# Token sums of a hybrid decoder layer taken from whole copies, two more pairs as block steps, weight sums and banks in another order

## The chip, the core and the metric

One Trainium2 chip, one core. The kernel is a whole decoder layer for 512 tokens, in float32. The time is that of the device for one execution, in microseconds (us); a median of three runs is given, and one further execution was profiled. TensorE (PE) multiplies, VectorE (DVE) and ScalarE (ACT) work on rows of up to 1024 elements in 128 partitions, GpSimd (POOL) does small things, SyncE (SP) issues most of the transfers. SBUF is the memory on the chip from which the engines read, PSUM the eight banks of 128x512 floats in which TensorE accumulates.

## What is computed

The reference, cut to what matters here:

```python
def rms_norm(x, g):
    y = x * lax.rsqrt(jnp.mean(x * x, axis=-1, keepdims=True) + RMS_EPS)
    return y * g

def swiglu(x, w_gate, w_up, w_down):
    return (jax.nn.silu(x @ w_gate) * (x @ w_up)) @ w_down

# the layer: x is 512 tokens x 1024, w_gate and w_up 1024 x 2816, w_down 2816 x 1024
x = x + 0.5 * rms_norm(swiglu(rms_norm(x, ffn1_pre), ...), ffn1_post)
x = x + rms_norm(mixer(rms_norm(x, mix_pre), ...), mix_post)
x = x + 0.5 * rms_norm(swiglu(rms_norm(x, ffn2_pre), ...), ffn2_post)
```

The mixer (two kinds of attention and gates) is not touched but for its last step, where its result is normed for the second FFN.

## The kernel before

**Products.** A float32 operand is split into a high part of TensorE's reduced float32 format and the rest: `whi`, `wlo` for weights, `xh`, `xl` for tokens. ScalarE casts the high part, VectorE subtracts it for the rest (`split`, L104 to L107). One product is three matmuls (`mm3`, L127 to L131): high by high, high by rest, rest by high.

**An FFN's up part.** The 2816 columns of w_gate and w_up are 22 blocks of 128, taken as 11 pairs p. A classical pair (`classical`, L390) is four units (gate and up of two blocks) of 8 slices of 128 of the inner dimension, three matmuls of 512 tokens each: 96 matmuls of 512 columns. A block pair (`strassen`, L325) takes gate and up together by seven products of half size after Strassen and Winograd: 7 x 2 x 4 x 3 = 168 matmuls of 256 columns. It needs sums of the weights (S1 to S4, 128x1024 on VectorE, from the tiles `raw`, into tiles `tmp`) and, once for each FFN, four sums of the tokens T1 to T4 (`token_sums`, L471). `STRASSEN` says which pairs are block pairs: before, 3 to 10 in the first FFN and 2 to 10 in the second.

**Token sums before.** T1 to T4 are sums and differences of four quarters of the normed tokens. Each quarter is first put together again from its parts, xh + xl, on VectorE (`join`, L491, eight times 128x512 for an FFN), then summed and split. `STEPS` deals the steps out over the classical blocks, from block 1 on.

**The start of an FFN.** The tokens are normed in four tiles t of 128 (`norm_steps`, L187): a scale on VectorE into `tmp`, eight 128x128 transposes on TensorE into two PSUM banks, a cast of each bank on ScalarE (xh) and a rest on VectorE (xl). The first four units, called g0, u0, g1, u1 here, are done in halves: first the tokens of tiles 0 and 1 (256 columns), later those of tiles 2 and 3, so that they can start early.

**What sets the order.** In the opening (L1426 to L1481) the order on ScalarE, VectorE and TensorE is that in which the code is written, with a few transposes of the identity (`keep_busy`) between. Elsewhere a scheduler orders the instructions within each engine. Each engine then runs its queue in order. PSUM banks are named by tags S (three buffers), T (two), V (one) and F (two); a bank that is given out anew can be written when all that read it have run. The tiles `raw`, into which weights are loaded, have three buffers, and a load starts when its buffer's last readers are done.

## Time and profile before

| what | before |
|---|---|
| median of 3 runs | 1138.97 us (1138.95 to 1139.98) |
| the profiled execution, its time | 1138.51 us |
| its span (first to last instruction) | 1136.4 us |
| TensorE busy | 1119.9 us, 6921 instructions |
| VectorE busy | 908.0 us, 1563 instructions |
| ScalarE busy | 638.0 us, 1145 instructions |
| pairs 0 to 10 of the first FFN, second halves on | from 26.69 us |
| second FFN, first matmul with its tokens | at 795.40 us |
| its pair 1 and pair 2, first matmul to first matmul | 820.46 to 842.24 and 842.24 to 862.40 us |

The times in a profile are counted from the start of the span. An entry of a timeline shows the start, the duration, the engine, the line of the kernel, the operation with output and input, and in brackets how long the engine stood idle before it and what ended that. Durations overlap a little, because an engine starts the next instruction before the last one has quite ended; so the distance from start to start is what one instruction costs in a row.

### The profile page before, as it was taken

How to read it: one execution, taken by the hardware profiler on the slowest of the kernel's cores; microseconds unless marked ns; L12 is line 12 of the kernel's file. 1: busy time of each engine (PE TensorE's matmuls, PEld its weight loads, DVE VectorE, ACT ScalarE, POOL GpSimd, SP SyncE). 2: the span in 40 equal slices, each digit the busy share in tenths (PEclk: the TensorE clock that was granted, in tenths of full speed). 3: DMA queues.
4: the chain of work that ended last, by engine and by line, in shares of the span. 5: the costliest groups of instructions: out<-in, count | busy, mean ns of one | idle time of the engine just before them, and what ended most of it. 6: DMA issues, size and time to landing. Idle time of an engine off the chain costs nothing.

```text
span 1136.4 us, 18463 instructions
## 1 busy us (share of the span) xinstructions
PE 1119.9 (99%) x6921; PEld 999.5 (88%) x6921; DVE 908.0 (80%) x1563; ACT 638.0 (56%) x1145; POOL 78.3 (7%) x112
## 2 busy tenths in 40 slices
PE   8999999999999999999999999999999999999997
PEld 7889999998878987778888998788989999998885
DVE  6989999878667889687665687976878888979665
ACT  5435555566464688687565635644445555558552
POOL 1000000000022032343000000001000000000001
PEclk9999999999999999999999999999999999999999
DMA  9995665578655552111476758683133433357753
GB/s 321 331 307 187 190 199 186 154 265 295 220 184 148 172 134 85 53 41 56 142 248 224 251 176 293 207 301 107 66 121 121 130 98 129 109 181 236 280 189 115
DMA packets 152908, 206.01 MB, mean 181 GB/s; under 512 B 19794, under 2 KB 97906, under 8 KB 152564
## 3 DMA queue, kind: packets, MB, share of 16 engines
q1 hardware_dynamic: 152816, 204.85, 55.1%
q8 instruction: 54, 0.88, 0.3%
q14 instruction: 34, 0.28, 0.1%
q10 hardware_dynamic: 4, 0.00, 0.0%
HBM read 165.45 MB, written 39.37 MB: 180 GB/s over the span
## 4 chain that ended last, share of the span: by engine, by line
PE 88%; DVE 6%; ACT 2%; DMA 1%; issue 1%; POOL 1%; SPq 0%; POOLq 0%; DVEq 0%; ACTq 0%
PE pb_F L131 11%; PE pb_F L129 11%; PE pb_F L130 11%; PE pb_S L131 8%; PE pb_S L130 8%; PE pb_S L129 8%; PE pb_T L130 6%; PE pb_T L131 6%; PE pb_T L129 6%; PE pb_V L130 3%; PE pb_V L129 3%; PE pb_V L131 3%; PE pb_V L986 2%; PE pb_T L971 1%; DVE SP_s L721 1%
## 5 line engine op out<-in xcount | busy, mean ns | idle before, releaser
L106 ACT CAST whi<-raw 128x1024 fp32r<-128x1024 f32 (+2 forms) x221 | 225.4, 1020 | 260.3 <-issue 68.2
L107 DVE TENSOR_TENSOR wlo<-raw,whi 128x1024 fp32r<-128x1024 f32 (+2 forms) x221 | 261.3, 1185 | 103.6 <-ACT whi L106 99.7
L129 PE MATMUL pb_F<-xh_t,whi 128*128 128x512 f32 (+1 forms) x392 | 142.6, 364 | 0.6 <-ACT whi L106 0.4
L131 PE MATMUL pb_F<-xh_t,wlo 128*128 128x512 f32 (+1 forms) x392 | 141.6, 361 | 0.5 <-DVE wlo L107 0.5
L130 PE MATMUL pb_F<-xl_t,whi 128*128 128x512 f32 (+1 forms) x392 | 141.9, 362 | 0.0
L106 ACT CAST whi<-tmp_t 128x1024 fp32r<-128x1024 f32 x51 | 53.5, 1048 | 61.0 <-PE pb_S L130 22.0
L131 PEld LDWEIGHTS pb_F<-xh_t,wlo 128*128 128x128 f32 x392 | 74.1, 189 | 10.8 <-DVE wlo L107 1.0
L129 PEld LDWEIGHTS pb_F<-xh_t,whi 128*128 128x128 f32 x392 | 74.1, 189 | 10.6 <-ACT whi L106 0.6
L130 PEld LDWEIGHTS pb_F<-xl_t,whi 128*128 128x128 f32 x392 | 74.2, 189 | 9.7
L107 DVE TENSOR_TENSOR wlo<-tmp_t,whi 128x1024 fp32r<-128x1024 f32 x51 | 62.4, 1223 | 25.2 <-ACT whi L106 23.9
L129 PE MATMUL pb_S<-xh_t,whi 128*128 128x256 f32 (+1 forms) x240 | 73.2, 305 | 0.0
L131 PE MATMUL pb_S<-xh_t,wlo 128*128 128x256 f32 (+1 forms) x240 | 73.0, 304 | 0.0
L130 PE MATMUL pb_S<-xl_t,whi 128*128 128x256 f32 (+1 forms) x240 | 73.0, 304 | 0.0
L151 POOL TENSOR_TENSOR rs_t<-rs_t,mhalf_t 128x1 f32<-128x1 f32 x24 | 19.2, 798 | 546.4 <-DVE rs_t L147 546.4
L130 PE MATMUL pb_T<-xl_t,whi 128*128 128x256 f32 (+1 forms) x184 | 53.9, 293 | 0.0
L129 PE MATMUL pb_T<-xh_t,whi 128*128 128x256 f32 (+1 forms) x184 | 53.9, 293 | 0.0
L131 PE MATMUL pb_T<-xh_t,wlo 128*128 128x256 f32 (+1 forms) x184 | 53.8, 292 | 0.0
L962 POOL TENSOR_SCALAR SP_s<-SP_s,st_t 128x384 f32<-128x384 f32 (+2 forms) x48 | 45.7, 968 | 106.5 <-DVE st_t L898 80.5
L130 PEld LDWEIGHTS pb_S<-xl_t,whi 128*128 128x128 f32 x240 | 45.9, 191 | 1.9
L129 PEld LDWEIGHTS pb_S<-xh_t,whi 128*128 128x128 f32 x240 | 45.9, 191 | 1.9
L131 PEld LDWEIGHTS pb_S<-xh_t,wlo 128*128 128x128 f32 x240 | 45.9, 191 | 1.9
L107 DVE TENSOR_TENSOR PT_s<-pb_T,PT_s 128x512 fp32r<-128x512 f32 (+1 forms) x72 | 39.2, 559 | 6.1 <-ACT PT_s L106 5.5
(808 smaller groups left out, 3350.6 us busy)
## 6 DMA issues: line engine op xcount, KB each, us to landing
raw<-in_ffn_w_up_dram SPq DMA_DIRECT2D x36, 512.0 KB, 5.2
raw<-in_w_in_dram SPq DMA_DIRECT2D x18, 1024.0 KB, 5.4
raw<-in_ffn_w_gate_dram SPq DMA_DIRECT2D x35, 512.0 KB, 4.7
raw<-tdram SPq DMA_DIRECT2D x16, 1024.0 KB, 5.2
raw<-in_ffn_w_down_dram SPq DMA_DIRECT2D x14, 1024.0 KB, 5.7
NN_s<-in_ffn_w_down_dram SPq DMA_DIRECT2D x22, 512.0 KB, 5.1
tdram<-NN_s SPq DMA_DIRECT2D x22, 512.0 KB, 3.9
raw<-tdram SPq DMA_DIRECT2D x8, 768.0 KB, 5.9
```

Source lines behind the costliest of these rows:

```text
L106: self.last_cast = self.nc.scalar.copy(dsthi, src).ins
L107: self.last_rest = self.nc.vector.tensor_sub(dstlo, src, dsthi.bitcast(F32)).ins
L129: mm(out, lhi, rhi, start=start, stop=False, skip_group_check=skip)
L130: mm(out, lhi, rlo, start=False, stop=False, skip_group_check=skip)
L131: mm(out, llo, rhi, start=False, stop=stop, skip_group_check=skip)
L151: nc.gpsimd.tensor_tensor(out=r, in0=v, in1=self.mhalf, op=OP.pow)
L721: nc.vector.tensor_tensor_reduce(p, s, w, -1.0, FLOOR, OP.add, OP.min, st_m)
L962: nc.gpsimd.tensor_scalar(pp, pp, st[:, 1, t:t + 1], None, op0=OP.mult)
L971: nc.tensor.transpose(b[:, o + (t - kk) * P:o + (t - kk + 1) * P], pt[pn][:, po + kk * P:po + (kk + 1) * P], self.ident)
L986: self.nc.tensor.matmul(out[:, kk * P:S], v, pp, start=first and kk == 0 and pi == 0, stop=False, skip_group_check=True)
```

## The change

Five things are changed.

1. **Whole copies.** In the opening and at the end of the mixer ScalarE copies each transposed bank into a slot as it stands (`full`, 128x256 twice for each bank, 16 copies for an FFN), tiles 0 and 1 into slots V and tiles 2 and 3 into slots x. The token sums are made from these copies, and the eight joins of each FFN go.
2. **Two more block pairs**: pair 2 in the first FFN, pair 1 in the second. The token sums are begun at block 0 instead of block 1, and `STEPS` deals them out faster.
3. **Weight sums in another order**: S3 = A11 - A21 first, S2 = A22 - S3, S1 = S2 + A11, then S4. Before, S1 = A21 + A22 came first, S2 = S1 - A11.
4. **Banks of pair 2 of the second FFN** are given out in another order.
5. The second FFN's count of banks starts at 3 instead of 7.

```diff
--- before.py
+++ after.py
@@ -44,14 +44,16 @@
 SPLIT_TAGS = dict(X=["Q"] * 4 + ["KA"] * 2, O=["V"] * 2 + ["KA"] * 2 + ["KB"] * 4 + ["SP"] * 11 + ["PT"] * 3,
                   Y=["PT"] * 5 + ["W"] * 2 + ["CB"] + ["Q"] * 4)
 T_TAGS = ["NN"] * 3 + ["N"] + ["PT"] * 8 + ["CB"]
-STRASSEN = range(3, NF // 2), range(2, NF // 2)
+STRASSEN = range(2, NF // 2), range(1, NF // 2)
 AHEAD = {0: 10, 1: 9}
 SUM_TAGS = {2: ["KB"] * 4, 3: ["x"] * 4, 4: ["x"] * 4, 5: ["V"] * 4, 6: ["x"] * 4, 7: ["V"] * 4,
             8: ["of"] * 2 + ["V"] * 2}
-STEPS = (0, 3, 3, 3, 3), (4, 4, 4)
+STEPS = (0, 4, 4, 4), (6, 6)
 HOLD_TAGS = ["W"] * 2 + ["Q"] * 4 + ["KA"] * 2 + ["V"] * 2 + ["CB", "ring"]
 PS_BUFS = dict(S=3, T=2, V=1, F=2)
 PS_TAGS = [t for t in PS_BUFS for _ in range(PS_BUFS[t])]
+
+WHOLE = "VV", "xx"
 
 OPEN = ("SS", "TT", "SS", "FF")
 AFTER_FFN, AFTER_MIX = ("SS", "FF", "SS", "TT"), ("SS", "TT", "FF", "SV")
@@ -63,6 +65,7 @@
         self.pool = ctx.enter_context(tc.tile_pool(name="sb", bufs=1))
         self.psum = ctx.enter_context(tc.tile_pool(name="ps", bufs=1, space=PSUM))
         self.nps = 0
+        self.whole = {}
         self.consts()
 
     def slot(self, tag, dt=F32, shape=(P, S)):
@@ -184,7 +187,10 @@
     def squares(self, t):
         return [self.meansq(x, S) for x in self.x[2 * t:2 * t + 2]]
 
-    def norm_steps(self, t, pre, tags):
+    def new_whole(self, half):
+        self.whole[half] = [[self.slot(tag).rearrange("p (k c) -> p k c", k=2) for _ in range(2)] for tag in WHOLE[half]]
+
+    def norm_steps(self, t, pre, tags, whole=False):
 
         nc = self.nc
         xn = self.sbt("tmp", [P, D], bufs=2)
@@ -207,12 +213,21 @@
         def rest(h):
             ks = slice(4 * h, 4 * h + 4)
             self.last_rest = nc.vector.tensor_sub(xl[:, ks, c], pt[h].rearrange("p (j c) -> p j c", j=4), xh[:, ks, c].bitcast(F32)).ins
-        return scale, transpose, cast, rest
-
-    def norm_T(self, t, pre, tags, sq=None):
+
+        def full(h):
+            if not whole:
+                return
+            if t % 2 == 0 and h == 0:
+                self.new_whole(t // 2)
+            for j in range(2):
+                o = self.whole[t // 2][h][j][:, :, (t % 2) * P:(t % 2 + 1) * P]
+                self.last_cast = nc.scalar.copy(o, pt[h][:, 2 * j * P:2 * (j + 1) * P].rearrange("p (j c) -> p j c", j=2)).ins
+        return scale, transpose, cast, rest, full
+
+    def norm_T(self, t, pre, tags, sq=None, whole=False):
 
         r = self.rstd(sq or self.squares(t))
-        scale, transpose, cast, rest = self.norm_steps(t, pre, tags)
+        scale, transpose, cast, rest, full = self.norm_steps(t, pre, tags, whole)
         for h in range(2):
             scale(h, r)
 
@@ -221,6 +236,8 @@
                 transpose(h)
                 cast(h)
                 rest(h)
+            for h in range(2):
+                full(h)
         return transposes
 
 
@@ -340,15 +357,16 @@
                  for i in (0, 4) for h in range(2)]
             b11, b21, b22 = x[0], x[2], x[3]
             t1, t2, t3, t4 = self.tsum
-            r12, r21, r11, r7 = [self.bank() for _ in range(4)]
-            nc.vector.tensor_add(s1, a21, a22)
+            banks = [self.bank() for _ in range(4)]
+            r12, r21, r11, r7 = [banks[i] for i in ((0, 3, 1, 2) if (n, p) == (1, 2) else range(4))]
             w = block(a11)
             nc.vector.tensor_sub(a21, a11, a21)
             product(r11, w, b11, True, False)
             w = block(a21)
             product(r7, w, t3, True, True)
-            nc.vector.tensor_sub(s2, s1, a11)
+            nc.vector.tensor_sub(s2, a22, a21)
             w = block(s2)
+            nc.vector.tensor_add(s1, s2, a11)
             nc.scalar.copy(r12, r11)
             product(r12, w, t2, False, False)
             w = block(a12)
@@ -400,11 +418,11 @@
                 bs.append(b)
             nc.scalar.activation(act, bs[0], AF.Silu)
             nc.vector.tensor_mul(act, act, bs[1])
-            if f == 1:
+            if f == 0:
                 sums.extend(self.token_sums())
-            if 1 <= f <= len(STEPS[n]):
+            if f < len(STEPS[n]):
                 with self.tc.issue_after(self.last_rest):
-                    for _ in range(STEPS[n][f - 1]):
+                    for _ in range(STEPS[n][f]):
                         sums.pop(0)()
 
         c = slice(0, H), slice(H, S)
@@ -472,7 +490,6 @@
 
 
         nc = self.nc
-        H = S // 2
         places = []
         for tag in T_TAGS:
             v = self.slot(tag, F32R, (P, D if tag == "NN" else S))
@@ -480,36 +497,27 @@
         self.tsum = [([], []) for _ in range(4)]
         steps = []
         for c in range(2):
-            hi, lo, whole = [[v.rearrange("p (k c) -> p k c", k=2) for v in g]
-                             for g in (places[8 * c:8 * c + 4], places[8 * c + 4:8 * c + 8],
-                                       [self.slot("x") for _ in range(4)])]
-            f1, f2, f3, f4 = whole
+            hi, lo = [[v.rearrange("p (k c) -> p k c", k=2) for v in g]
+                      for g in (places[8 * c:8 * c + 4], places[8 * c + 4:8 * c + 8])]
+            whole = f1, f2, f3, f4 = [self.whole[h][i][c] for i, h in ((0, 0), (1, 1), (0, 1), (1, 0))]
             for i in range(4):
                 for o, v in zip(self.tsum[i], (hi[i], lo[i])):
                     o.extend(v[:, k] for k in range(2))
 
-            def join(dst, i, h, c=c):
-                ks, cs = slice(4 * i + 2 * c, 4 * i + 2 * c + 2), slice(h * H, (h + 1) * H)
-                nc.vector.tensor_add(dst, self.xht[:, ks, cs].bitcast(F32), self.xlt[:, ks, cs].bitcast(F32))
-
             def sub(dst, x, y):
                 nc.vector.tensor_sub(dst, x, y)
 
             def parts(i, hi=hi, lo=lo, whole=whole):
                 self.split(hi[i], lo[i], whole[i])
 
-            def s1(f1=f1, f3=f3, join=join):
-                join(f3, 0, 1)
-                join(f1, 0, 0)
+            def s1(f1=f1, f3=f3):
                 sub(f1, f3, f1)
 
-            def s2(f1=f1, f2=f2, f3=f3, join=join):
-                join(f2, 1, 1)
+            def s2(f1=f1, f2=f2, f3=f3):
                 sub(f3, f2, f3)
                 sub(f2, f2, f1)
 
-            def s3(f2=f2, f4=f4, join=join):
-                join(f4, 1, 0)
+            def s3(f2=f2, f4=f4):
                 sub(f4, f4, f2)
 
             steps += [s1, s2, lambda p=parts: p(0), s3, lambda p=parts: (p(1), p(2)), lambda p=parts: p(3)]
@@ -1438,8 +1446,8 @@
             sq0 = [sq, self.meansq(self.x[1], S)]
             sq1 = self.squares(1)
             r0 = self.rstd(sq0)
-            scale0, transpose0, cast0, rest0 = self.norm_steps(0, g, OPEN[0])
-            scale1, transpose1, cast1, rest1 = self.norm_steps(1, g, OPEN[1])
+            scale0, transpose0, cast0, rest0, full0 = self.norm_steps(0, g, OPEN[0], True)
+            scale1, transpose1, cast1, rest1, full1 = self.norm_steps(1, g, OPEN[1], True)
             hi, lo = self.wpair([KT, P])
             src = self.pre_raw["g"][:, :, 0:P]
 
@@ -1473,15 +1481,19 @@
             cast1(1)
             rest1(1)
             self.pre_split = [self.ktiles(w) for w in ((hi, lo), self.wsplit(self.pre_raw["u"][:, :, 0:P], [KT, P]))]
+            full0(0)
             sq2 = self.squares(2)
+            full0(1)
             self.pre_split.append(self.ktiles(self.wsplit(self.pre_raw["g"][:, :, P:2 * P], [KT, P])))
-            t2 = self.norm_T(2, g, OPEN[2], sq2)
+            t2 = self.norm_T(2, g, OPEN[2], sq2, True)
+            full1(0)
             sq3 = self.squares(3)
+            full1(1)
             self.pre_split.append(self.wslots(self.pre_raw["u"][:, :, P:2 * P], "SP"))
-            t3 = self.norm_T(3, g, OPEN[3], sq3)
+            t3 = self.norm_T(3, g, OPEN[3], sq3, True)
         self.pending = [t2, t3]
 
-        def boundary(post, pre, store, tags=None):
+        def boundary(post, pre, store, tags=None, whole=False):
             def load():
                 return self.gains((post, pre))
 
@@ -1492,14 +1504,14 @@
                 if pre is not None:
                     if t == 0:
                         self.new_xT()
-                    self.pending.append(self.norm_T(t, gain, tags[t]))
+                    self.pending.append(self.norm_T(t, gain, tags[t], None, whole))
             return load, finish
 
         self.ffn(0, a["ffn1_w_gate"][0], a["ffn1_w_up"][0], a["ffn1_w_down"][0],
                  *boundary(a["ffn1_post"][0], a["mix_pre"][0], self.xdram, AFTER_FFN), a["x"][0], "TTSV", 6, self.distances)
-        self.mixer(*boundary(a["mix_post"][0], a["ffn2_pre"][0], self.x2dram, AFTER_MIX))
+        self.mixer(*boundary(a["mix_post"][0], a["ffn2_pre"][0], self.x2dram, AFTER_MIX, True))
         self.ffn(1, a["ffn2_w_gate"][0], a["ffn2_w_up"][0], a["ffn2_w_down"][0],
-                 *boundary(a["ffn2_post"][0], None, out), self.x2dram, "TTFS", 7)
+                 *boundary(a["ffn2_post"][0], None, out), self.x2dram, "TTFS", 3)
 
 
 _INS = ['x', 'ffn1_pre', 'ffn1_post', 'ffn1_w_gate', 'ffn1_w_up', 'ffn1_w_down',
```

How this moves the instructions is seen in the order on the engines. ScalarE in the opening, **before**, from the last cast of the first two tiles on; `xh_t` is the cast of tokens, `whi` that of weights (u0, then g1), ACTIVATE the squares of tiles 2 and 3, `SP_s` the cast of u1:

```order
L205 CAST xh_t<-pb_T 128x4x128
L106 CAST whi<-raw 128x1024
L138 ACTIVATE junk_t,ss_t<-x_s 128x512 x2
L106 CAST whi<-raw 128x1024
L138 ACTIVATE junk_t,ss_t<-x_s 128x512 x2
L106 CAST SP_s<-raw 128x512 x2
```

The same place **after**, where the COPY rows at L224 are the whole copies of tile 0 (from the banks S) and tile 1 (from the banks T):

```order
L211 CAST xh_t<-pb_T 128x4x128
L109 CAST whi<-raw 128x1024
L224 COPY V_s<-pb_S 128x2x128 x2
L141 ACTIVATE junk_t,ss_t<-x_s 128x512 x2
L224 COPY V_s<-pb_S 128x2x128 x2
L109 CAST whi<-raw 128x1024
L224 COPY V_s<-pb_T 128x2x128 x2
L141 ACTIVATE junk_t,ss_t<-x_s 128x512 x2
L224 COPY V_s<-pb_T 128x2x128 x2
L109 CAST SP_s<-raw 128x512 x2
```

Eight copies have come between the casts and the squares; the first copy out of a bank T stands behind the cast of g1.

TensorE at the first matmul of unit g0, with what each row waits for in brackets, **before** (the transposes of the identity at L1424 are those of `keep_busy`; the numbers name the buffers):

```order
L1424 MATMUL pb_V_90<-ident_t_61 128x128 x4
L129 MATMUL pb_T_226<-xh_t_88,whi_133 128x256 [waits DVE_49]
L130 MATMUL pb_T_226<-xl_t_89,whi_133 128x256
L131 MATMUL pb_T_226<-xh_t_88,wlo_134 128x256
L129 MATMUL pb_T_226<-xh_t_88,whi_133 128x256
```

and **after**:

```order
L1432 MATMUL pb_V_90<-ident_t_61 128x128 x4
L132 MATMUL pb_T_238<-xh_t_88,whi_133 128x256 [waits DVE_49,Activation_49]
L133 MATMUL pb_T_238<-xl_t_89,whi_133 128x256
L134 MATMUL pb_T_238<-xh_t_88,wlo_134 128x256
L132 MATMUL pb_T_238<-xh_t_88,whi_133 128x256
```

The rows are the same; the first matmul now waits for ScalarE's counter (Activation) as well as for VectorE's. The count that it waits for is reached with the second copy out of the bank T that the unit is given.

VectorE at the start of the second FFN, **before**: `rs_t` is a step of tile 3's norm, `tmp_t<-x_s,rs_t,CP_s` its two scales, `xl_t` the rests of tiles 2 (F) and 3 (S, V), and L493 the first joins.

```order
L147 TENSOR_SCALAR rs_t<-ss_t 128x1
L197 SCALAR_TENSOR_TENSOR tmp_t<-x_s,rs_t,CP_s 128x512 x2
L209 TENSOR_TENSOR xl_t<-pb_F,xh_t 128x4x128 x2
L209 TENSOR_TENSOR xl_t<-pb_S,xh_t 128x4x128
L209 TENSOR_TENSOR xl_t<-pb_V,xh_t 128x4x128
L493 TENSOR_TENSOR x_s<-xh_t,xl_t 128x512 x3
```

The same place **after**:

```order
L150 TENSOR_SCALAR rs_t<-ss_t 128x1
L363 TENSOR_TENSOR raw<-raw 128x1024
L203 SCALAR_TENSOR_TENSOR tmp_t<-x_s,rs_t,CP_s 128x512 x2
L367 TENSOR_TENSOR tmp_t<-raw 128x1024
L215 TENSOR_TENSOR xl_t<-pb_F,xh_t 128x4x128 x2
L215 TENSOR_TENSOR xl_t<-pb_S,xh_t 128x4x128
L215 TENSOR_TENSOR xl_t<-pb_V,xh_t 128x4x128
```

Two sums of weights have come into the sequence: pair 2's S3 (L363) ahead of tile 3's scales, and pair 1's S2 (L367) ahead of the rests.

## The prediction

> **What bounds the kernel now.** I read the page's busy line first, then the windows view of TensorE for the two long stretches in which the FFNs' up products run.
>
> ```profile
> PE 1119.9 (99%) x6921; PEld 999.5 (88%) x6921; DVE 908.0 (80%) x1563; ACT 638.0 (56%) x1145; POOL 78.3 (7%) x112
> ...
> 20.00:337.00 317.00, 316.56 (x2101) 1.00 0.70 233
> 803.00:1117.00 314.00, 314.00 (x2165) 1.00 0.45 150
> ```
>
> The columns of the lower rows are the stretch, its length, TensorE's busy time with its instruction count, granted clock, DMA share, GB/s. TensorE is busy 316.56 of 317 us and 314.00 of 314. So it sets the end nearly everywhere, and two things follow. A matmul that is removed from these stretches shortens the run by its whole length. And a pause that is put in ahead of them lengthens it by its whole length, since nothing behind it has room to catch up. The few gaps at the start therefore matter as much as the matmuls, and I looked at the timeline there next.
>
> **The gain: two pairs as block steps.** The change takes pair 2 of the first FFN and pair 1 of the second from the classical form (96 matmuls of 512 columns) to the block form (168 of 256). The second FFN runs one of each kind back to back, cut exactly at their first matmuls:
>
> ```profile
> 820.46:842.24 21.78, 21.78 (x98) 18.03 (x97) 17.08 (x24) 7.04 (x10) 0.00 (x0) 1.00 0.42 136
> 842.24:862.40 20.16, 20.16 (x170) 20.15 (x169) 17.61 (x20) 10.74 (x14) 0.00 (x0) 1.00 0.28 95
> ```
>
> Behind the length stand TensorE, weight loads, VectorE, ScalarE, GpSimd, clock, DMA share and GB/s. The classical pair takes 21.78 us, the block pair 20.16, with TensorE busy throughout in both. One pair gained is 1.62 us, two are **−3.2 us**. VectorE has 17.61 us of work in a block pair of 20.16, ScalarE 10.74, so in the steady state both stay hidden. The eight removed joins and the added copies of the token sums lie on these two engines and cost or gain nothing by themselves where TensorE does not wait for them. The reordered weight sums (S2 and S1 swap, one input is awaited less) are the same number of VectorE instructions per pair, so I put them at nothing; 2.5 us of slack per pair covers them.
>
> **The opening: the first matmul gets a new thing to wait for.** This is the term I found only by following the banks. Here is the opening of before, ScalarE and then TensorE (start, duration, line, operation, and in brackets the idle time ahead):
>
> ```profile
> 12.14 1.06 ACT L106 CAST whi<-raw 128x1024 fp32r<-128x1024 f32 x1
> 13.10 0.64 ACT L138 ACTIVATE junk_t<-x_s 128x512 bf16<-128x512 f32 x1
> ...
> 14.39 0.18 ACT L138 ACTIVATION_READ_ACCUMULATOR junk_t<-x_s 128x1 f32 x1
> 15.04 1.05 ACT L106 CAST whi<-raw 128x1024 fp32r<-128x1024 f32 x1 [0.46 <-DMA raw<-in_ffn_w_gate_dram]
> 15.99 0.62 ACT L138 ACTIVATE junk_t<-x_s 128x512 bf16<-128x512 f32 x1
> ```
> ```profile
> 11.43 0.60 PE L1424 MATMUL pb_V<-ident_t 128*128 128x128 f32 x4
> 12.03 0.39 PE L129 MATMUL pb_T<-xh_t,whi 128*128 128x256 f32 x1
> ...
> 18.00 0.28 PE L131 MATMUL pb_T<-xh_t,wlo 128*128 128x256 f32 x1
> 18.93 1.31 PE L202 MATMUL pb_S<-ident_t,tmp_t 128*128 128x128 f32 x8 [0.65 <-DVE tmp_t L197]
> ```
>
> The first unit accumulates in a bank T that held half of the second tile's transposes. In before, that bank is free when VectorE has taken its rest, and the matmul starts at 12.03, right behind the keep-busy transposes. After the change the copies of the whole sums read the same bank, and TensorE's first matmul waits on ScalarE too, for the second copy out of that bank. ScalarE works in order, and ahead of this copy now stand: the cast of u0 (ends so that the next starts at 13.10), two copies out of S, two squares, two more copies out of S, the cast of g1, then the two copies out of T.
>
> A copy of 128x256 out of PSUM by ScalarE has near relatives in before:
>
> ```profile
> L106 ACT CAST PT_s<-pb_T 128x256 fp32r<-128x256 f32 x32 | 11.5, 370 | 7.3 <-DVE PT_s L107 3.8 <-PE pb_T L1237 2.3 <-PE pb_T L971 1.0
> 382.08 0.70 ACT L106 CAST PT_s<-tmp_t 128x248 fp32r<-128x248 f32 x2
> ```
>
> One takes 0.37 us from PSUM; two of about this size, from SBUF, take 0.70 back to back (so they overlap by some 0.1). I take 0.65 for two, with 0.50 and 0.74 as ends. The walk along ScalarE: 13.10 + 0.65 = 13.75; the two squares last from 13.10 to 14.57 in before, 1.47, which gives 15.22; + 0.65 = 15.87 (the load of g1, which came at about 15.04, is there by now); the cast 15.04 to 15.99 is 0.95, so 16.82; + 0.65 = **17.5**. TensorE's first matmul starts 5.5 us later than 12.03.
>
> What of this comes back: the 48 matmuls in the two T banks ran from 12.03 to 18.12 and then waited 0.65 for the scaled tile 2. They would now take 5.8 to 6.1 us from 17.5, to 23.3 or 23.6. The second T bank's copies stand behind two more squares, at about 17.5 + 1.4 + 0.65 = 19.6, and are needed at 17.5 + 2.9 = 20.4, so they hold nothing. Tile 2's scale moves to about 20, earlier than needed. The transposes that started at 18.93 start at about 23.4: **+4.5 us** (4.0 with the low copy price, 4.8 with the high). From there TensorE has the same work as before, and no gap into which the delay could vanish.
>
> **The clock during that pause.** TensorE would sit idle for 5.5 us, from 12.03 on. The trace shows one such pause, behind the last matmul of the run, and the slow start of the run:
>
> ```profile
> 1129.56 0.39 PE L131 MATMUL pb_T<-whi,PT_s 128*128 128x512 f32 x1
> 1130.00:1134.00 4.00, 0.00 (x0) 0.00 (x0) 2.23 (x4) 0.69 (x2) 0.55 (x1) 1.00 0.31 115
> 1134.00:1136.40 2.40, 0.00 (x0) 0.00 (x0) 0.00 (x0) 0.00 (x0) 0.00 (x0) 0.52 0.30 114
> 6.69 1.97 PE L202 MATMUL pb_S<-ident_t,tmp_t 128*128 128x128 f32 x8 [0.41 <-DVE tmp_t L197]
> 10.85 0.75 PE L202 MATMUL pb_T<-ident_t,tmp_t 128*128 128x128 f32 x4
> ```
>
> The last matmul ends at 1129.95; the granted clock is 1.00 up to 1134 and 0.52 after it, which is half rate from about 1134.1, so 4.15 us after the last matmul. A pause of 5.5 us is longer than that, and the rate would fall at about 16.2. At the start, four transposes took about 1 us at 6.69 (eight in 1.97) and 0.75 at 10.85: some 4 us of nearly steady work until the full rate came. I take 3.9 us at half rate from 17.5, of which half is lost: **+1.9 us**. The ends are nothing (the rate stays) and 3.9 (two such stretches). This does not hang on the sum above.
>
> [...]
>
> **The start of the second FFN.** The copies of tiles 0 and 1 fall into idle time of ScalarE. But pair 2's block subtraction of the raw weights (which in before is pair 2's first sum too, and much later in VectorE's order since pair 1 was classical) now stands ahead of tile 3's scale.
>
> ```profile
> 794.72 0.38 SPq L335 DMA_DIRECT2D raw<-in_ffn_w_gate_dram  x1
> 795.17 0.49 SPq L335 DMA_DIRECT2D raw<-in_ffn_w_up_dram  x1
> raw<-in_ffn_w_gate_dram SPq DMA_DIRECT2D x1, 512.0 KB, 3.8
> raw<-in_ffn_w_up_dram SPq DMA_DIRECT2D x1, 512.0 KB, 5.8
> 800.19 0.21 DVE L147 TENSOR_SCALAR rs_t<-ss_t 128x1 f32<-128x1 f32 x1 [0.95 <-ACT junk_t L138]
> 801.13 1.41 DVE L197 SCALAR_TENSOR_TENSOR tmp_t<-x_s,rs_t,CP_s 128x512 f32<-128x512 f32 x2 [0.73 <-POOL rs_t L151]
> 802.03 0.60 PE L202 MATMUL pb_S<-ident_t,tmp_t 128*128 128x128 f32 x4
> 802.60 0.66 PE L202 MATMUL pb_V<-ident_t,tmp_t 128*128 128x128 f32 x4
> ```
>
> The load of that raw tile hangs on the same event as in before (the last rest of unit u1), is issued at 795.17 and lands 5.8 us later, at 801.0. The subtraction of 128x1024 takes about 1.15 us until the next instruction, so the scale starts at 802.15 instead of 801.13. Its two halves end at about 802.9 and 803.5, and TensorE's transposes into S and V, at 802.03 and 802.60 in before, wait for them: they are through at 804.0 instead of 803.0. Next, a 128x1024 sum for pair 1 stands ahead of tile 2's rest, and unit g1's bank waits for the rest and two copies, about 806.1, while the 14 matmuls of u1 that are ahead of it are done at 805.8. Together **+1.3 us**; nothing if the load lands before 799.9, 2.0 if it comes 0.7 later. A shift of the whole stretch, from the opening, does not change it, because the loads shift along.
>
> **Pair 2 of the first FFN** is the place that I cost at nothing. There, the DMA share is 0.91 between 38.20 and 81.76, and in VectorE's order a subtraction on pair 3's raw weights stands between the rests of pair 2's fourth and fifth products.
>
> ```profile
> 38.20:81.76 43.56, 24.91 (x65) 12.10 (x65) 1.00 0.91 308
> 73.20 1.22 DVE L344 TENSOR_TENSOR tmp_t<-raw 128x1024 f32<-128x1024 f32 x1 [2.00 <-DMA raw<-in_ffn_w_up_dram]
> ```
>
> In before VectorE waited 2.00 us for such a load, and TensorE did not notice. After the change TensorE comes there 4.5 to 6.4 us later while the loads are mostly tied to other loads and stores, which covers the wait; without that cover it costs up to 2.0.
>
> **The sum.** −3.2 + 4.5 + 1.9 + 1.3 = +4.5 us on the profiled execution of 1138.51 (span 1136.4 and 2.1 around it): **1143.0 us**. The median of the three runs is 0.46 above that execution; this is inside the range and I add nothing for it. A measurement of this kernel can tell about 0.2%, 2.3 us, from no change.
>
> **The rivals.**
> 1. *The clock does not fall.* The pause then costs only its 4.5 us: −3.2 + 4.5 + 1.3 = +2.6, or **1141.1**, which is 0.19% above the median of before: not slower by what can be told. [...] If the second FFN's load also comes in time it is 1139.8.
> 2. *The first matmul is not held, and the two pairs are all gain*: 1138.5 − 3.2 + 1.3 at most, **1135.3 to 1136.6**. For it speaks that the bank and its wait are read from the program and no trace shows them. Against it: even if the copies cost no time, the wanted copy stands behind the cast of g1, which ends at 16.0 in before; the matmul would come 4.0 later, 3.3 net of the 0.65 gap, and so still eat the gain.
> 3. *Both new waits and the load of pair 3 bite*: VectorE's 2.0 at pair 2 becomes TensorE's, or the half rate lasts for a second stretch: **1144.9 to 1147**.
> 4. *The change does not do what it says*: a converted pair does not run at 20.16 because its token sums (T3 first, T2 next) or its weight sums come late. Each such pair loses its 1.6: 1144.6 to 1146.2. Against it, the sums start one step earlier than in before.
>
> **How the numbers follow.** Forecast 0.47 (1142.0 to 1144.5); rival 1 0.30 (1139.6 to 1142.0), of which 0.20 lies below 1141.25, the 0.2% line; rival 2 0.06; rival 3 0.12; rival 4 0.05. The range 1139.6 to 1145.4 leaves out rival 2 and about half of 3 and 4, some 0.15. Faster by over 0.2% is rival 2 alone, 0.06; within 0.2% is 0.20 of rival 1 with a little of the forecast's low end, 0.22; slower 0.72.
>
> **What would show it.** TensorE's first matmul with xh should start at about 17.5, released by a ScalarE copy, with an idle of some 5 us ahead of it; the 256-column matmuls behind it should stand 0.21 to 0.24 us apart for some 4 us instead of 0.12, or the clock did not fall; tile 2's transposes should have no gap ahead. The block subtraction near 801 should be released by a DMA and tile 3's scale come about 1 us later than the squares ask. The converted pairs should last 20.2 us. I am wrong if the first matmul starts near 12, if the pause is absorbed further on, or if pair 2 of the first FFN shows TensorE waiting for VectorE.

## The result, and the profile after

The changed kernel takes 1147.13 us (median of 4 runs, 1145.8 to 1147.9) beside 1139.22 for the kernel of before; the ratio is 1.0067 (95% interval 1.0052 to 1.0081), and the medians are 7.9 us apart. Forecast were 1143.0 with a range of 1139.6 to 1145.4. The direction and the place of the largest loss were right; the time lies above the range, because a second loss had been put at nothing. The profiled execution took 1145.8 us with a span of 1143.6, 7.2 more than before.

The page's busy line of the changed kernel, and the view of its waits on TensorE (who waited for whom: us in total, times, longest):

```profile
PE 1119.1 (98%) x7065; PEld 1005.0 (88%) x7065; DVE 914.4 (80%) x1567; ACT 656.7 (57%) x1193; POOL 81.4 (7%) x112
```
```profile
PE pb_T L132 <- ACT V_s L224: 5.6, 1, 5.6
PE pb_S L1280 <- DVE PT_s L110: 2.1, 2, 1.6
PE pb_S L208 <- DVE tmp_t L203: 2.0, 4, 0.7
...
PE pb_S L134 <- DVE wlo L110: 0.9, 1, 0.9
PE pb_T L134 <- DVE wlo L110: 0.7, 2, 0.3
```

The first row of waits is the forecast one: a matmul on a bank T that waits for a whole copy. But there are two rows, `wlo` under L134 with banks S and T, that the same list of the kernel before (down to 0.2 us) does not have: TensorE waits for the rests of block products. To see where the 7.2 us came in, the starts of the same matmuls in the two traces:

| TensorE's first matmul of | before, us | after, us | later by |
|---|---|---|---|
| first FFN, pair 1 | 38.21 | 43.14 | 4.93 |
| first FFN, pair 3 | 81.76 | 86.82 | 5.06 |
| first FFN, pair 10 | 222.87 | 229.24 | 6.37 |
| second FFN, unit g0 | 795.40 | 802.60 | 7.20 |
| second FFN, second halves | 808.94 | 817.30 | 8.36 |
| second FFN, pair 2 | 842.24 | 848.98 | 6.74 |

From row to row, the opening lost 4.93. Pair 2 of the first FFN gained nothing (0.13 lost where 1.6 should have been gained), and pairs 3 to 9 lost 1.3. Another 0.83 came between pair 10 and the second FFN, and 1.16 at the second FFN's start. There pair 1 gained its 1.62. The last 0.5 up to 7.2 came behind the block pairs of the second FFN.

**The opening.** The timelines of ScalarE and of TensorE, and the clock in one-microsecond windows (columns as in the prediction):

```profile
14.68 0.63 ACT L224 COPY V_s<-pb_S 128x256 f32<-128x256 f32 x2
15.20 1.05 ACT L109 CAST whi<-raw 128x1024 fp32r<-128x1024 f32 x1
16.14 0.66 ACT L224 COPY V_s<-pb_T 128x256 f32<-128x256 f32 x2
```
```profile
10.63 0.60 PE L1432 MATMUL pb_V<-ident_t 128*128 128x128 f32 x4
16.85 0.58 PE L132 MATMUL pb_T<-xh_t,whi 128*128 128x256 f32 x1 [5.62 <-ACT V_s L224]
```
```profile
12.00:13.00 1.00, 0.00 (x0) 0.00 (x0) 1.00 (x3) 1.00 (x3) 0.00 (x0) 1.00 1.16 321
13.00:14.00 1.00, 0.00 (x0) 0.00 (x0) 1.00 (x2) 1.00 (x4) 0.00 (x0) 0.66 1.22 293
...
19.00:20.00 1.00, 1.00 (x6) 1.00 (x6) 1.00 (x3) 0.74 (x2) 0.00 (x0) 0.50 1.06 389
20.00:21.00 1.00, 1.00 (x9) 1.00 (x9) 1.00 (x3) 0.00 (x0) 0.00 (x0) 0.93 1.07 389
```

The matmul starts as the second copy out of T ends, with 5.62 us of idle time (forecast 5.5), and the clock is at half from about 13.3 to 20.1. The matmuls of 256 columns stand 0.21 us apart up to there and 0.12 behind it.

**The block pairs.** Windows cut at the first matmuls of pair 1, 2, 3 and 8 of the first FFN and of pair 1 of the second:

```profile
43.14:64.92 21.78, 21.78 (x98) 18.02 (x97) 20.93 (x33) 7.05 (x10) 1.58 (x2) 1.00 0.91 308
64.92:86.82 21.90, 20.66 (x170) 20.25 (x169) 18.17 (x22) 10.32 (x13) 0.00 (x0) 1.00 0.87 278
86.82:107.26 20.44, 20.44 (x171) 20.27 (x170) 19.59 (x26) 10.89 (x15) 0.00 (x0) 1.00 0.63 204
187.90:208.70 20.80, 20.45 (x170) 20.25 (x169) 19.26 (x25) 10.89 (x15) 0.00 (x0) 1.00 0.60 187
828.82:848.98 20.16, 20.16 (x170) 20.16 (x169) 16.67 (x19) 9.24 (x12) 0.00 (x0) 1.00 0.38 118
```

In the second FFN the converted pair lasts 20.16 us, as worked out. In the first, the converted pair 2 lasts 21.90, no better than a classical one, and block pairs behind it (3 and 8 are shown) have become longer than the 20.16 that all of them took before. What TensorE waits for there, VectorE and TensorE in pair 2:

```profile
70.47 1.23 DVE L110 TENSOR_TENSOR wlo<-raw,whi 128x1024 fp32r<-128x1024 f32 x1
75.32 1.23 DVE L363 TENSOR_TENSOR raw<-raw 128x1024 f32<-128x1024 f32 x1 [3.62 <-DMA raw<-in_ffn_w_up_dram]
76.46 1.22 DVE L110 TENSOR_TENSOR wlo<-tmp_t,whi 128x1024 fp32r<-128x1024 f32 x1
```
```profile
77.73 0.39 PE L134 MATMUL pb_S<-NN_s,wlo 128*128 128x256 f32 x1 [0.90 <-DVE wlo L110]
```

L363 is S3 = A11 - A21 of the **next** pair. VectorE reaches it, stands 3.62 us for its load, and only then makes the rest that pair 2's fifth product needs; TensorE waits 0.90 for it, and 0.34 more for the rest of the sixth product: VectorE has 18 to 20 us of work in a pair of 20, so it catches up slowly.

**The second FFN's start**, where tile 3's scale was to wait:

```profile
807.37 0.21 DVE L150 TENSOR_SCALAR rs_t<-ss_t 128x1 f32<-128x1 f32 x1 [0.95 <-ACT junk_t L141]
807.57 1.23 DVE L363 TENSOR_TENSOR raw<-raw 128x1024 f32<-128x1024 f32 x1
809.24 1.41 DVE L203 SCALAR_TENSOR_TENSOR tmp_t<-x_s,rs_t,CP_s 128x512 f32<-128x512 f32 x2 [0.44 <-POOL rs_t L154]
```
```profile
810.05 0.66 PE L208 MATMUL pb_S<-ident_t,tmp_t 128*128 128x128 f32 x4 [0.66 <-DVE tmp_t L203]
```

S3's load was there in time (its row shows no wait). The scale comes 1.87 us after `rs_t` instead of 0.94 (801.13 from 800.19), so 0.93 later. S3 on VectorE alone would account for only some 0.4 of it: VectorE is free for the next instruction at 808.7, and at the old distance the scale was due at 808.3. But the scale waits 0.44 more, for GpSimd, whose step between `rs_t` and the scale became longer. Here it is before and after:

```profile
800.55 0.55 POOL L151 TENSOR_TENSOR rs_t<-rs_t,mhalf_t 128x1 f32<-128x1 f32 x1 [2.75 <-DVE rs_t L147]
```
```profile
807.73 1.48 POOL L154 TENSOR_TENSOR rs_t<-rs_t,mhalf_t 128x1 f32<-128x1 f32 x1 [2.75 <-DVE rs_t L150]
```

The same step takes 0.93 us more while S3 runs beside it, and these 0.93 are the whole delay.

### The profile page after: what moved, and what is told of

Read it like the earlier page. It is cut to its first block, busy times and chain, and to the rows that moved or that the text cites. A ratio compares the mean times of both kernels' runs of the same rounds, so it can differ in the third digit from the quotient of the medians.

```text
span 1143.6 us, 18825 instructions
## 1 busy us (share of the span) xinstructions
PE 1119.1 (98%) x7065; PEld 1005.0 (88%) x7065; DVE 914.4 (80%) x1567; ACT 656.7 (57%) x1193; POOL 81.4 (7%) x112
## 4 chain that ended last, share of the span: by engine, by line
PE 79%; DVE 10%; DMA 3%; ACT 3%; issue 3%; POOL 1%; SPq 0%; DVEq 0%; POOLq 0%; ACTq 0%
PE pb_F L134 10%; PE pb_F L132 10%; PE pb_F L133 10%; PE pb_S L134 6%; PE pb_S L132 6%; PE pb_S L133 6%; PE pb_T L133 5%; PE pb_T L134 5%; PE pb_T L132 5%; DVE wlo L110 2%; PE pb_V L133 2%; PE pb_V L132 2%; PE pb_V L134 2%; PE pb_V L994 2%; PE pb_T L979 1%
## 5 line engine op out<-in xcount | busy, mean ns | idle before, releaser
L134 PE MATMUL pb_F<-xh_t,wlo 128*128 128x512 f32 (+1 forms) x392 | 140.9, 359 | 0.5 <-DVE wlo L110 0.5
L133 PE MATMUL pb_F<-xl_t,whi 128*128 128x512 f32 (+1 forms) x392 | 141.1, 360 | 0.0
L109 ACT CAST whi<-tmp_t 128x1024 fp32r<-128x1024 f32 x57 | 59.8, 1050 | 51.1 <-PE pb_S L133 17.6
L110 DVE TENSOR_TENSOR wlo<-tmp_t,whi 128x1024 fp32r<-128x1024 f32 x57 | 69.6, 1221 | 24.4 <-ACT whi L109 24.1
L134 PEld LDWEIGHTS pb_F<-xh_t,wlo 128*128 128x128 f32 x392 | 74.1, 189 | 10.5 <-DVE wlo L110 1.0
L134 PE MATMUL pb_S<-xh_t,wlo 128*128 128x256 f32 (+1 forms) x232 | 67.5, 291 | 0.1
L132 PE MATMUL pb_S<-xh_t,whi 128*128 128x256 f32 (+1 forms) x232 | 67.5, 291 | 0.0
L133 PE MATMUL pb_S<-xl_t,whi 128*128 128x256 f32 (+1 forms) x232 | 67.3, 290 | 0.0
L154 POOL TENSOR_TENSOR rs_t<-rs_t,mhalf_t 128x1 f32<-128x1 f32 x24 | 20.1, 836 | 546.1 <-DVE rs_t L150 546.1
L132 PE MATMUL pb_T<-xh_t,whi 128*128 128x256 f32 x184 | 52.9, 287 | 5.6 <-ACT V_s L224 5.6
L134 PE MATMUL pb_T<-xh_t,wlo 128*128 128x256 f32 x184 | 52.8, 287 | 0.3 <-DVE wlo L110 0.3
L133 PE MATMUL pb_T<-xl_t,whi 128*128 128x256 f32 x184 | 52.7, 287 | 0.0
L134 PEld LDWEIGHTS pb_S<-xh_t,wlo 128*128 128x128 f32 x232 | 44.4, 192 | 1.1 <-DVE wlo L110 0.5
```

The source lines that it names most:

```text
L109: self.last_cast = self.nc.scalar.copy(dsthi, src).ins
L110: self.last_rest = self.nc.vector.tensor_sub(dstlo, src, dsthi.bitcast(F32)).ins
L132: mm(out, lhi, rhi, start=start, stop=False, skip_group_check=skip)
L133: mm(out, lhi, rlo, start=False, stop=False, skip_group_check=skip)
L134: mm(out, llo, rhi, start=False, stop=stop, skip_group_check=skip)
L154: nc.gpsimd.tensor_tensor(out=r, in0=v, in1=self.mhalf, op=OP.pow)
```

## The experiments

The theory after this reading: the opening costs about 5 us; the order of the weight sums costs the rest, because S3 of the next pair stands in VectorE's queue ahead of rests that are due, with a load still under way.

**The changed kernel again**, beside the others:

> The changed kernel once more, beside the other runs, for a comparison on the same chip at the same time. Theory (nothing else differs): 1145.8 to 1147.9 as in its first four runs. Rival (the 1.5 us by which the variants with an earlier or warmer opening came out below it were differences between measurements): 1145.2 to 1145.8 here.

Measured: 1146.3 us (1144.58 to 1148.3), ratio 1.0061 (1.0047 to 1.0075). The first measurement holds, and the rival's range is missed. Its own profile differs from the first one in an instructive way: pair 2 lasted 20.15 us here, since the load that S3 waits for landed earlier (VectorE stood 1.80 us instead of 3.62), but pairs 3 to 9 gave 2.5 us back in the same manner (every wait of TensorE there is for a rest), and pair 10 starts at 228.65. So the loss is larger where the load lands later, and it differs from run to run; so does the time, over 3.7 us.

**The copies alone**: block pairs and sums of before, whole copies as changed.

```diff
-STRASSEN = range(2, NF // 2), range(1, NF // 2)
+STRASSEN = range(3, NF // 2), range(2, NF // 2)
...
+            nc.vector.tensor_add(s1, a21, a22)
...
-            nc.vector.tensor_sub(s2, a22, a21)
+            nc.vector.tensor_sub(s2, s1, a11)
...
-            nc.vector.tensor_add(s1, s2, a11)
```

> The whole copies alone: the changed kernel with the weight sums of before and the block pairs of before (3 to 10 and 2 to 10). Theory (the copies cost the opening 5.3 us, a half clock included, and the second FFN's start 0.3, and without the conversions nothing comes back): 5.5 us above before, 1144.2 to 1145.2, first matmul at about 17, no waits for rests in the first FFN's block pairs. Rival (the freed 5 us of joins on VectorE per FFN give part of it back): below 1143.5.

Measured: 1144.76 us, ratio 1.0046 (1.0032 to 1.006), as forecast by the theory: the first matmul at 17.29, and all block pairs of the first FFN at 20.15 or 20.16. Taking the joins off VectorE gives nothing back. The new order and count of banks (items 4 and 5 of the change) are still in this kernel and were not taken out alone; its second FFN loses nothing at its start (13.58 us from the first matmul to the second halves, 13.54 before), so they do no harm there.

**The copies of tile 1 early**: out of the T banks right behind their casts, tile 0's later.

```diff
...
             rest1(1)
+            self.early = True
+            self.new_whole(0)
+            full1(0)
             self.pre_split = [...]
-            full0(0)
+            full1(1)
             sq2 = self.squares(2)
-            full0(1)
...
-            full1(0)
+            full0(0)
             sq3 = self.squares(3)
-            full1(1)
+            full0(1)
```

> The changed kernel, with tile 1's whole copies moved right behind its casts and tile 0's to where tile 1's were. Theory (the opening's loss is the first matmul's wait for ScalarE and the half clock that follows): the idle time ahead of the first matmul falls from 5.62 us to about 1, the granted clock stays at 1.00 behind it, the second halves of the first units start near 27.3 instead of 31.62, and the run takes 4.3 us less, about 1142.8. Rival (the transfers of the first FFN set the pace from pair 2 on, and the late start only hid that): TensorE meets the same loads earlier, pair 2 of the first FFN lasts 24 us or more instead of 21.9, and the run stays at 1145 to 1147.

Measured: 1145.45 us, ratio 1.005 (1.0035 to 1.0065). The opening did nearly what the theory said: the first matmul starts at 13.42 after a wait of 0.37, and pair 1 at 39.42 instead of 43.14. (The clock column shows no fall here, but the matmuls stand 0.21 us apart, as in the changed kernel at half clock, up to about 14.65, and 0.12 behind it.) But the end hardly moved. The same two pairs as above (the window of pair 2; VectorE's wait inside it; TensorE's wait in that window):

```profile
61.21:84.88 23.67, 21.88 (x169) 21.67 (x168) 19.95 (x24) 10.22 (x13) 0.00 (x0) 0.93 0.84 274
```
```profile
72.50 1.22 DVE L365 TENSOR_TENSOR raw<-raw 128x1024 f32<-128x1024 f32 x1 [3.60 <-DMA raw<-in_ffn_w_up_dram]
```
```profile
PE pb_S L135 <- DVE wlo L111: 1.8, 1, 1.8
```

Pair 2 now lasts 23.67 us and pair 3 22.26, and pair 10 starts at 229.89, later than the changed kernel's 229.24. TensorE came 3.7 us earlier, the load only about 2.8. The wait grew from 0.90 and 0.34 to 1.79 us, and behind it the clock is at half for 3.4 us, from about 76.1 to 79.5 (mean 0.93 in the window), which costs about another 1.7 (0.07 of the 23.67). The rival was right about what happens; whether it was right about why (the transfers themselves) the sums had to tell.

**The clock held up** by 46 more transposes of the identity during the pause:

```diff
-BUSY = 4, 2, 2, 4
+BUSY = 4, 2, 2, 50
```

> The changed kernel with 46 more keep-busy transposes ahead of the first matmul, on the bank that they already use. Theory (the fall of the clock during the pause costs 1.6 us of the opening): the first matmul starts at the same time, about 16.9, the clock is 1.00 throughout, the 48 matmuls behind it take 5.8 us instead of 7.3, and the run takes about 1.5 us less, 1145.6. Rival (transposes do not hold the clock up, or the later scale of tile 2 hides the slow matmuls): within 0.5 us of the changed kernel's 1147.1.

Measured: 1145.55 us, ratio 1.005 (1.0035 to 1.0065); against the changed kernel's two medians that is 0.8 to 1.6 less, and the intervals overlap. In the profile the clock stays at 1.00 through the pause, and the 48 matmuls take 5.85 us instead of 7.29. So the transposes held the clock here, and the half rate had cost 1.4 us. Since the first matmul came 0.3 later here (17.16), pair 1 starts 1.1 earlier, at 42.03 instead of 43.14 (or 43.07 in the second profile). The waits for rests come all the same: pair 2 takes 20.15 us here, but pairs 3 to 9 take 144.2. Pair 10 starts at 228.15, 1.1 earlier than in the first profile of the changed kernel and 0.5 earlier than in the second.

**The weight sums in the order of before**, all else as changed (the diff of the copies alone, without its first pair of lines):

> The changed kernel with the weight sums in the order of before (S1 = A21 + A22 first). Theory (the new first sum S3 = A11 - A21 stands ahead of the preceding pair's rests in VectorE's order and waits there for a load, so that TensorE runs dry): the waits of TensorE for VectorE's rests at pair 2 (0.90 and 0.34 us) and in the pairs behind it (0.2 to 0.35 each) go, tile 3's scale in the second FFN is no longer delayed by 0.93, and the run takes 2.5 to 4 us less, 1143.1 to 1144.6. Rival (the load is simply too late for whichever sum comes first): the waits stay and the run is at 1146.5 to 1147.5.

Measured: 1142.91 us, ratio 1.0032 (1.002 to 1.0043), 3.4 to 4.2 less than the changed kernel and a little below the theory's range. The opening is as bad as ever (the first matmul at 17.23), but pair 2 is whole:

```profile
65.37:85.52 20.15, 20.15 (x169) 20.15 (x168) 18.27 (x23) 10.34 (x13) 0.00 (x0) 1.00 0.95 306
```

All pairs behind it take 20.16, and the second halves of the second FFN lose 0.25 instead of 1.16. The DMA share is higher than in the changed kernel's pair 2 (0.95 against 0.87), so the transfers were not too slow for this pair. The rival falls: the same loads are early enough when the sum that asks for them stands behind the rests that are due.

**The new sums with S3 held back** behind the rest of its own pair's first block:

```diff
-            nc.vector.tensor_sub(a21, a11, a21)
+            with self.tc.issue_after(self.last_rest):
+                nc.vector.tensor_sub(a21, a11, a21)
```

> The changed kernel with its own new weight sums, but S3 held behind the rest of its own pair's first block in VectorE's order. Theory (the place in the order does the harm, not the other arithmetic): as with the sums of before, 1142 to 1144, no waits of TensorE for rests in the first FFN's block pairs. Rival (the new arithmetic, with fewer sums alive early, or the in-place S3 does it): it stays above 1145.5.

Measured: 1143.3 us, ratio 1.0033 (1.002 to 1.0046), and every block pair of the first FFN at 20.15 or 20.16. Pair 2's window, the rest of its fifth product and the next pair's S3 (L364 here) in that run:

```profile
65.27:85.42 20.15, 20.15 (x169) 20.15 (x168) 16.68 (x21) 10.33 (x13) 0.00 (x0) 1.00 0.99 324
```
```profile
72.23 1.23 DVE L110 TENSOR_TENSOR wlo<-tmp_t,whi 128x1024 fp32r<-128x1024 f32 x1 [0.78 <-ACT whi L109]
82.56 1.22 DVE L364 TENSOR_TENSOR raw<-raw 128x1024 f32<-128x1024 f32 x1
```

The rest no longer stands behind a load, and S3, 10 us later, finds its load there. In the block pairs the new arithmetic is harmless; the place of S3 in VectorE's queue is what costs. The second FFN's start, too, is as before: GpSimd's step takes 0.55 us and the second halves come 13.57 us after the first matmul.

**The new sums alone**, in the kernel of before:

```diff
-            nc.vector.tensor_add(s1, a21, a22)
...
-            nc.vector.tensor_sub(s2, s1, a11)
+            nc.vector.tensor_sub(s2, a22, a21)
             w = block(s2)
+            nc.vector.tensor_add(s1, s2, a11)
```

> The kernel of before with nothing changed but the order of the weight sums (S3 first). Theory (this part alone is harmful: S3 can go as soon as one weight tile is there, is put ahead of the preceding pair's rests and waits for its load): TensorE waits for rests at several block pairs of the first FFN, 1 to 5 us in all, and the run is 2 to 6 us above before, 1141 to 1145. Rival (it is harmful only together with pair 2's conversion and the denser loads there): within 0.8 us of before, 1138.5 to 1140.

Measured: 1141.23 us, ratio 1.0017 (1.0009 to 1.0026). Neither expectation held in full. The run is 2.2 us slower, but only two pairs of the first FFN are longer, at 20.31, together 0.3 us. In the second FFN the start costs 0.86 (14.40 us from the first matmul to the second halves instead of 13.54), with GpSimd's step at 1.39 beside S3. The rest of the profile's 2.1, 0.45 in the opening and 0.5 behind the last block pair, is not explained. So in the first FFN the harm is larger with the conversion and the denser loads; in the second it is there with the new sums alone.

**Pair 2 of the first FFN classical again**, all else as changed:

```diff
-STRASSEN = range(2, NF // 2), range(1, NF // 2)
+STRASSEN = range(3, NF // 2), range(1, NF // 2)
```

> The changed kernel with pair 2 of the first FFN classical again, all else as changed. Theory (pair 2 as block steps gains 1.62 us and loses about 1.7 to waits): the run stays within 0.5 us of 1147.1. Rival (the conversion gains its 1.6 and the waits would come in any case, at the next pair): 1148.5 to 1149.

Measured: 1145.12 us, ratio 1.0047 (1.0032 to 1.0062): 1.2 to 2 below the changed kernel, with overlapping intervals and below both ranges. As changed, the conversion of pair 2 brought nothing and may have cost. Here pairs 3 to 9 lose 0.7 in the profile, less than with the conversion, so the rival's waits came only in part.

**Early copies and one or the other order together:**

> Both repairs together: tile 1's whole copies early in the opening, and the weight sums in the order of before. Theory (the new place of the first weight sum is what ate the opening's gain in the run with the early copies, where pair 2 and the pairs behind it waited 6 us for VectorE's rests): those waits are gone, both conversions count with 1.6 us each, the opening costs about 1.1 and the second FFN's start 0.3, so the run is 1.5 to 2 us below the kernel of before, 1137.2 to 1138. Rival (the loads themselves pace the first FFN as soon as TensorE comes early): pair 2 of the first FFN shows waits of 1 us or more and the run is at 1139.5 to 1142.

> Early copies and the held S3 together. Theory: like the early copies with the sums of before, 1137 to 1138.5, below the kernel of before. Rival (held back so far, S3 and S2 come late for the second and third product): waits of TensorE for rests at the second product of each block pair, and 1140 or more.

Measured: with the sums of before 1140.19 us, ratio 1.0012 (1.0002 to 1.0021): not below before, the rival's numbers. Pair 2 takes 23.69 us there, and VectorE waits for a load again, now with S1 (L363 in that kernel), since TensorE comes early:

```profile
60.84:84.53 23.69, 21.16 (x170) 20.35 (x168) 20.59 (x24) 11.27 (x14) 0.00 (x0) 1.00 0.86 286
```
```profile
75.30 1.23 DVE L363 TENSOR_TENSOR tmp_t<-raw 128x1024 f32<-128x1024 f32 x1 [2.95 <-DMA raw<-in_ffn_w_up_dram]
```

With S3 held back it is 1137.66 us, ratio 0.999 (0.998 to 0.9999): pair 2 takes 20.91, and the waits of TensorE for rests are gone from it; what is left is one of 0.5 us for ScalarE. With the sums of before, the late opening gave the load time; with the early one, S1 stands in the way as S3 did. Held behind the rest, S3 does not.

**Is pair 2's conversion worth something then?** The last kernel with pair 2 classical (the range edit above):

> Early copies and held S3, but pair 2 of the first FFN classical again. Theory (the conversion of pair 2 brings 0.8 of its 1.6 us, the other half goes to waits for its first products' inputs): 0.8 us more than with the conversion, 1138 to 1138.8. Rival 1 (it brings the full 1.6): 1139 to 1139.6. Rival 2 (it brings nothing): 1137.3 to 1137.9.

Measured: 1138.04 us, ratio 0.999 (0.9981 to 0.9999). Against 1137.66 the conversion brings 0.4 us by the medians and 0.85 by the windows (20.91 against 21.76). The intervals don't tell the theory from rival 2; the full 1.6 is seen in neither number.

**The first unit in another bank**: early copies and held S3, and g0 put into the third bank of S, which no transpose of the opening uses.

```diff
-... a["x"][0], "TTSV", 6, self.distances)
+... a["x"][0], "STTV", 6, self.distances)
```

> The best so far (early copies, S3 held), and the first unit g0 put into the third bank of S, which no transposes use, with u0 and g1 in T. Theory (the rest of the opening's loss, 1.0 us, is still the wait for the copies out of T): the first matmul has no wait for a copy, starts at 12.0 to 12.4, and the run is 0.7 to 1.1 us lower than with the early copies and the held S3 alone, 1136.5 to 1137.2. Rival (ScalarE is now the bound of the opening: the copies push the casts of u0 and g1, and the same time is lost a little later): within 0.4 us of 1137.7.

Measured: **1135.87 us**, ratio 0.9972 (0.9961 to 0.9983), the best of all and 3.3 us below before, more than the theory gave. The window of its pair 2:

```profile
59.50:79.65 20.15, 20.15 (x169) 20.15 (x168) 19.38 (x24) 10.26 (x13) 0.00 (x0) 1.00 0.91 301
```

No matmul waits for a copy any more. TensorE starts on g0 at 11.24, earlier than the theory said, and pair 1 starts at 37.71, half a microsecond before the kernel of before. Against the profile with the early copies and the held S3 alone, the opening gives 1.6 us, pair 2 0.75 and the stretch with the mixer 0.6. Pair 2 has its full gain although TensorE arrives earliest of all; why its wait of 0.5 is gone too was not tested, and the stretch with the mixer differs between profiles anyway (see the end of the next section).

The lengths of the first FFN's pairs in the profiles, from first matmul to first matmul:

| kernel | pair 1 starts | pair 2 | pairs 3 to 9 together | median, us |
|---|---|---|---|---|
| before | 38.21 | 21.76 (classical) | 141.1 | 1139.2 |
| changed | 43.14 | 21.90 | 142.4 | 1147.1 |
| changed, second profile | 43.07 | 20.15 | 143.6 | 1146.3 |
| copies alone | 44.64 | 21.76 (classical) | 141.1 | 1144.8 |
| early copies | 39.42 | 23.67 | 145.0 | 1145.5 |
| clock held up | 42.03 | 20.15 | 144.2 | 1145.6 |
| sums of before | 43.58 | 20.15 | 141.1 | 1142.9 |
| S3 held | 43.48 | 20.15 | 141.1 | 1143.3 |
| new sums alone | 38.66 | 21.76 (classical) | 141.4 | 1141.2 |
| pair 2 classical | 42.99 | 21.76 (classical) | 141.8 | 1145.1 |
| early, sums of before | 39.05 | 23.69 | 141.2 | 1140.2 |
| early, S3 held | 39.33 | 20.91 | 141.1 | 1137.7 |
| early, S3 held, pair 2 classical | 38.90 | 21.76 (classical) | 141.1 | 1138.0 |
| early, S3 held, g0 in S | 37.71 | 20.15 | 141.1 | 1135.9 |

The runs were measured in four groups; the kernel of before, measured in each, had medians of 1139.0 to 1139.5.

## Why the prediction was wrong

**The gain, −3.2.** Half of it came: the second FFN's pair 1 took 20.16 us as worked out. In the first FFN the profile shows 21.90 for pair 2, nothing gained. That a pair *can* take 20.15 there is shown by four of the experiments and by the changed kernel's second profile.

**The opening, +4.5, and the clock, +1.9.** Mechanism and place were right: the bank, the copy, the pause of 5.62 us against 5.5, and a clock that falls in it. Together they were put at 6.4 and measured 4.93 at the start of pair 1. By the run with the clock held up, 3.8 of that is the pause and 1.1 the clock, so each term was too large. The queue on ScalarE started 0.35 us earlier in this execution (u0's cast at 11.79 instead of 12.14), two copies took 0.53 from start to start instead of 0.65, and the half rate lasted 3.3 us behind the first matmul instead of 3.9. The clock fell in every profile with the late first matmul (mean granted clock 0.993 to 0.996) but the one with the added transposes (0.999). It need not fall, though: in three of the four executions of the copies alone, and in one of four in the second measurement of the changed kernel, the mean granted clock is 0.999 as in before, which leaves room for at most 3.4 us at half rate in the whole run (a mean of 0.9985 or more over some 1143 us). So rival 1's condition, or something near it, does occur. Its gain does not show in the time: those three executions of the copies alone took 1144.2 to 1145.0 us, the profiled one, with the fall, 1144.7. What the fall costs a whole execution therefore stays open.

**The second FFN's start, +1.3**: 1.16 from the first to the second halves. The size was right, by luck in part, since the reason was not: the load was in time, S3 in VectorE's queue alone would have cost the scale some 0.4, and the delay of 0.93 came from GpSimd's step of 0.55 us, which took 1.48 beside S3. The prediction did not have this step.

**The step that failed** is the sentence "The reordered weight sums ... I put them at nothing". I counted VectorE's instructions and its slack, 2.5 us in a pair, and did not ask where in the queue the first of the sums stands and for what it waits. S3 needs only the first weight tile, so the order puts it early, ahead of rests of the pair that runs, and its wait holds them up. In pair 2 that cost 1.74 us (21.90 against 20.16), in pairs 3 to 9 1.3 in the profile of the result and 2.5 in the second one. The runs with S3 elsewhere show it: 141.1 for these pairs, as before, with S3 held and with the sums of before. Holding S3 is worth about 3 us with the late opening, and about 7 with the early one (from 5.9 above the kernel of before, measured beside it, to 1.3 below).

I had the place in view, as the pair that I "cost at nothing" and as rival 3, and gave VectorE's wait there up to 2.0 us; it was 3.62. My reason for zero, that a late TensorE gives the loads time, was not wrong as a mechanism (with the early copies TensorE's wait in pair 2 grows from 1.24 to 1.79 us), but 4.9 us were not enough, and I looked for it at one pair only, where every block pair of the first FFN has the same S3. Rival 3's range, 1144.9 to 1147, holds the profiled 1145.8, but partly by luck: it counted pair 2 alone, and an opening larger than the measured one.

**What stays open.** 0.8 us of the profile's 7.2 came between pair 10 of the first FFN and the second FFN, where in the mixer a wait for `PT_s` behind a late load took 1.6 us instead of 0.5. This wait is 0.5 in all four profiles with the sums of before; with the new sums it is 0.5 to 2.1, and the longest is with S3 held. So S3's place ahead of the rests is not its cause; whether the new sums are in some other way is not shown. The 0.5 us at the very end is also open: from the end of the last block pair to the end of the span every other profile takes 113.1 to 113.3 us, the kernel of before 112.7 in its one profile.

## What to carry to other kernels

When an instruction gets a new reader of a shared buffer, follow the buffer to its next writer: the copy out of a PSUM bank was cheap here (two took 0.53 us), but the next user of the bank waited 5.62 us for all that stood ahead of the copy in its engine's queue. When sums or other preparations are put in another order, ask of the first one what it needs and how early a scheduler may place it; here S3 could go early but waited 3.62 us for a load, and held up the rests due behind it on an engine with 18 to 20 us of work in a pair of 20; its busy share, 80%, said nothing of that. And a repair at the start of a pipeline can be taken back further on by such a wait (the early copies alone brought pair 1 forward by 3.7 us and pair 10 not at all), so the two must be tried together before either is judged.
